# Retention scores with full-height matmuls: the queries' low parts kept per head beside rows of zeros

## The chip, the core and the metric

The kernel runs on one core of a Trainium2 chip. The metric is the device time of one execution in microseconds (us), as the median of several runs. The engines are named as the profile names them: PE is TensorE (matmuls), PEld its weight loads, DVE VectorE, ACT ScalarE, POOL GpSimd, SP the engine that issues the transfers.

## The reference

A model of three blocks over 512 tokens of width 1024: a layer of forgetting attention, a layer of retention, and a block of dilated attention, convolution and feed-forward. The change touches the retention alone, cut here to what matters (12 heads, keys and queries of 64, values of 128):

```python
qf = rotary(q.reshape(B, S, H, dk).astype(jnp.float32), pos)
kf = rotary(k.reshape(B, S, H, dk).astype(jnp.float32), pos) * (dk ** -0.5)
...
inner = jnp.einsum('bhnd,bhmd->bhnm', qc, kc) * d_inner[None]
o = jnp.einsum('bhnm,bhme->bhne', inner, vc)
```

The kernel computes the chunks' recurrence as one causal product over all 512 tokens: scores of every key block against the queries behind it, times a table of decays, then times the values.

## The kernel before

Every float32 product is made of float32r parts, a high part and a low part that holds the rest: hi by hi, hi by lo, lo by hi. The helper `mm3` writes these three matmuls (L213, L214, L215), and `add_nat` the same three in another layout (L422 to L424). Slots of 128 x 512 come from `arena_r` (50, float32r) and `arena_f` (23, float32), PSUM banks from a ring of eight; the slot that has been free longest is handed out first.

Jobs stand in a list, each with a tile of weights. Between two pieces of a job's foreground work (24 or 48 matmuls of a projection) the driver lets one or two steps of background chains run. A head of the retention is such a chain, `push_head`, with the steps `s1` (scores), `s2` (product with the values, by the helper `pv`), `s2b` (sums of squares, a small POOL power at L231, diagonal blocks at L251) and `s3` (the norm spread by two matmuls, L261 and L262, and the gate). A scheduler then orders the instructions of each engine.

A pair of heads shares one projected chunk. `store_rot` turns it by the rotary tables (ACT L1087, DVE L1088, POOL L1089, DVE L1090) and stores parts: of a key, for each head, the high part in the head's own 64 partitions with the low part in the other 64; of a query, for each head, the high part in both halves, and one slot for the low parts of both heads, each in its own 64 partitions. So the first matmul of a score block (L1127, 128 partitions) gives hi by hi and lo by hi at once, and the second (L1128) adds hi by lo over the head's 64 partitions alone. A group of scores is eight matmuls, four blocks of two: 512, 384, 256 and 256 columns. DVE multiplies each block with the decays (L1131, L1136), ACT makes its high part (L1132), POOL its low part (L1133), and `s2` reads them.

Of the kernel before, what the change touches and what calls it, by code (L numbers as in the profile page):

```python
# [11 lines left out]
F32 = mybir.dt.float32  # L12
# [28 lines left out]
class Slots:  # L41
    """Equal pieces of one on-chip buffer, handed out in program order, the longest free one first."""
# [26 lines left out]
class HL:  # L69
    """A float32 array held as the sum of two float32r arrays."""  # L70
# [10 lines left out]
class Job:  # L81
    """One weight tile: how to load it, how to cut its split, and the pieces of work that use it."""
# [6 lines left out]
class Chain:  # L89
    """Steps of background work, in order; one at most between two pieces of the foreground."""  # L90
# [10 lines left out]
def tile_kernel(ctx: ExitStack, tc: tile.TileContext, a: dict, out: bass.AP, stop_at=None):  # L101
    nc = tc.nc
# [21 lines left out]
    # ---------------------------------------------------------------- constants  # L124
# [53 lines left out]
    def vec_steps(r0, r1):  # L178
        """Rows r0 .. of the vectors, turned so that their elements lie on partitions, as steps."""
        n = r1 - r0  # L180
        d = {}

        def load():
            d["t"] = st = FS.get()
            r = 0
            while r < n:
                ap, i = vrows[r0 + r]
                m = 1
                while r + m < n and vrows[r0 + r + m] == (ap, i + m):
                    m += 1  # L190
                nc.sync.dma_start(st[r : r + m, 0:P], ap[i : i + m, :])
                r += m

        def turn():
            pt = PA.get()
            nc.tensor.transpose(pt[:, 0:n], d["t"][0:n, 0:P], ident[0:n, 0:n])
            nc.vector.tensor_copy(vec[:, r0:r1], pt[:, 0:n])
            pt.free()
            d["t"].free()

        return [load, turn]

    # ---------------------------------------------------------------- small helpers
# [4 lines left out]
    def mm3(ps, pairs, start=True, stop=True, check=True):  # L208
        """ps (+)= sum of w.T @ x, each float32 operand as hi + lo."""
# [7 lines left out]
    def stat_mm(ps4, src, first, last, blocks=range(4)):  # L217
        """ps4[t, i] += sum over partitions of src[:, 128 i + t]."""
# [14 lines left out]
    def bcast(ps, col4, n=4):  # L233
        """ps[:, t] = the value of token t, on every partition."""
        for i in range(n):
            nc.tensor.matmul(  # L236
                ps[:, i * P : (i + 1) * P],
                col4[:, i : i + 1].to_broadcast([P, P]),
                ident,
                start=True,  # L240
                stop=True,
            )

    def diag(col4):
        """Four diagonal blocks of the values of 512 tokens, split."""
# [13 lines left out]
    def bcast_r(ps, g):  # L259
        """ps[:, t] = the sum over the partitions of g[:, t], on every partition."""  # L260
# [4 lines left out]
    def norm_apply(xs, g0, rb, dst, cs=range(KC)):  # L265
        """dst[c] = split of xs[c] * g * rb."""
# [16 lines left out]
    # ---------------------------------------------------------------- the driver  # L283
# [22 lines left out]
    def pump():  # L306
        """Loads as far ahead as the buffers allow."""
# [8 lines left out]
    def cut(j):  # L316
        """The next piece of the split of j's weights into hi and lo."""
# [15 lines left out]
    def cut_ahead(i, n):  # L333
        """Up to n pieces of the split, of the tiles up to i + 2."""
# [47 lines left out]
    A = slice(None)  # L382
# [8 lines left out]
    def add_proj(w, c0, x, evacs, n=512):  # L391
        """Two 128-wide column chunks of x @ w, transposed; evacs[i](psum) stores chunk i."""
# [17 lines left out]
    def add_nat(w, c0, x, evac, nb=4, cut=None):  # L410
        """x @ w[:, c0:c0+256] in its natural layout; evac(b, psum) stores rows 256 b .. 256 b + 255."""
# [22 lines left out]
    def add_acc(w, r0, nr, ncols, xs, evac, cols=None):  # L434
        """Chunks of xs' rows r0.. of w: partial products of w's rows, transposed; evac(f, psum)."""
# [22 lines left out]
    # ---------------------------------------------------------------- attention pieces  # L458
    def softmax_T(blocks, dst):
        """Transposes of blocks: dst list of (psum column, source) per psum bank."""  # L460
# [4 lines left out]
    # ================================================================ phase: start  # L465
    G = {}

    def load_nat(src, nt, between=lambda: None):
        """[128 nt, 1024] in its natural layout: units [token block][column half]."""
# [8 lines left out]
    def nat_rstd(r, nt, act):  # L478
        """Root mean square of each row -> [128, 4] of 1 / rms."""
# [18 lines left out]
    def mem_steps(layer):  # L498
        """Split of mem * g, transposed, and 1 / rms of mem's rows, as steps."""
# [55 lines left out]
    def x_steps():  # L555
        """The residual and h, transposed, from x, as steps."""
# [41 lines left out]
    def sq_add(key, c, src, scale=1.0):  # L598
        """Sums of squares over the chunks."""
# [14 lines left out]
    def spread_to(key, col4):  # L614
        """Broadcast of [128, 4] to a unit."""
# [6 lines left out]
    def raw_split(c, g0):  # L622
        """Split of x * g, which still lacks 1 / rms."""
# [6 lines left out]
    def norm_steps(g0, key="sq", keep_rb=False):  # L630
        """New h from the residual x, whose squares are summed up, as steps."""
# [31 lines left out]
    # ================================================================ mem attention  # L663
# [45 lines left out]
    def store_q(key, first=None):  # L709
        """Split of a chunk; its first 128 tokens whole as well."""  # L710
# [98 lines left out]
    def add_out(layer, g, then=None):  # L809
        """Residual += o[4g .. 4g+3] @ w_out rows; then(f) follows each chunk."""  # L810
# [44 lines left out]
    # ================================================================ layer 0  # L855
    def add_fox():
# [3 lines left out]
        def ev_f(ps):  # L860
            """Cumulated log-sigmoid of the forget logits, times -sqrt(128), to DRAM."""
# [91 lines left out]
        def f_unit(h, l):  # L953
            """Rows 0 .. 31: products of hi and of x's lo; rows 32 .. 63: of the weights' lo, which lie beside hi."""
# [80 lines left out]
    def tr_causal(p, p33):  # L1035
        """p[i]: [128 queries of block i, keys 0 .. 128 (i + 1)], transposed and split.

        keys 0, queries 0:512; keys 1, queries 128:512; keys 2, queries 256:512, lo beside hi; p33: keys 3, whole."""
# [15 lines left out]
    def pv(v, odd, pt, p33):  # L1054
        """Output, transposed: sum over key blocks of v.T @ pt; the last block, 128 queries, as plain float32."""
# [13 lines left out]
    # ================================================================ layer 1  # L1069
    def add_ret():  # L1070
# [9 lines left out]
        def store_rot(key):  # L1080
            """Rotated pair of heads: a key's hi beside its lo, a query's hi twice; last the queries' lo."""

            def f(ps):
# [8 lines left out]
                n = 2 if key[0] == "k" else 3  # L1092
                G[key] = r = [RS.get() for _ in range(n)]
                for i in range(2):
                    own, other = HEADS[i], HEADS[1 - i]
                    nc.scalar.copy(r[i][own], t[own])
                    if n == 3:
                        nc.scalar.copy(r[i][other], t[own])
                    lo = r[i][other] if n == 2 else r[2][own]
# [7 lines left out]
        def push_head(h):  # L1107
# [5 lines left out]
            def s1():  # L1113
                q, k = G[("q", h // 2)], G[("k", h // 2)]
                rows = HEADS[h % 2]
                kh, qh, ql = k[h % 2], q[h % 2], q[2]
# [5 lines left out]
                for j in range(4):  # L1122
# [5 lines left out]
                    nc.tensor.matmul(ps[:, 0:n], kh[rows, sl], ql[rows, q0:512], start=False, stop=True)  # L1128
# [107 lines left out]
    # ================================================================ block 2  # L1236
# [10 lines left out]
    def bias_steps():  # L1247
        """Bias of every head by distance, masked distances at -1e30, reversed, times sqrt(128), to DRAM."""
# [41 lines left out]
    def mid_steps():  # L1290
        """h = rmsnorm(rmsnorm(x, final), mix_pre); then the inner norm, which is the residual, to DRAM."""
# [43 lines left out]
    def glu_evac(i, gate, val, c, raw):  # L1335
        """Gated value chunk c into a padded row; raw ones still lack h's 1 / rms."""
# [10 lines left out]
    def add_glu_raw():  # L1347
        """Chunks 0 and 1 of the gated value, from h without its 1 / rms."""
# [86 lines left out]
    def add_qk(g, j):  # L1435
        """Query and key chunk of head 4 g + j."""
# [33 lines left out]
    def by_residue(ap):  # L1470
        """Tokens 4 t + r of a row of 512 in the order of (r, t)."""
        return ap.rearrange("p (t r) -> p r t", r=4)

    def stats(j, g):
        """Row maxima (columns 0 .. 11) and sums (12 .. 23) of the three groups, for tokens in the order of group g."""
# [5 lines left out]
    def own_exp(g, j, p):  # L1481
        """Exponentials over the group's own maxima, and their sums."""
# [9 lines left out]
    def scores_dil(g, j):  # L1492
        """A dilated group attends within the tokens of equal residue by 4, in blocks of 128."""
# [41 lines left out]
    def push_softmax(j):  # L1535
        def swap():
            """Each order's maxima and sums to the other, by DRAM."""
# [12 lines left out]
        def coef(g):  # L1550
            """Columns 0 .. 11: exp(own maximum - joint maximum) over the joint sum."""
# [74 lines left out]
    def tr_band(p):  # L1626
        """p[0]: [128, keys 0]; p[i]: [128, keys i - 1, i].  Two split units of two key blocks each;
        key block j: queries 128 j .. 128 j + 255, the last one zeros and then queries 384:512."""
# [33 lines left out]
    def add_v2(g, jp):  # L1662
        """Values of two heads; those of a dilated group go through DRAM into the order of (residue, token)."""
# [24 lines left out]
    def conv_norm():  # L1688
        """LayerNorm over channels, silu and split of the convolution's output; pushed as background steps."""
# [53 lines left out]
    def add_block2():  # L1743
# [123 lines left out]
        def last(hf):  # L1867
            """Chunks 6 and 7 for 256 of the tokens."""
# [16 lines left out]
        def post(hf):  # L1885
            """The residual and its raw split, for 256 of the tokens."""
# [32 lines left out]
    # ================================================================ feed-forward  # L1919
    def add_ffn():  # L1920
# [38 lines left out]
        def add_up_raw():  # L1959
            """Chunks 0 to 3 of the gated unit, from h without its 1 / rms; the first four products side by side."""  # L1960
# [63 lines left out]
        def down(g, lo, n):  # L2024
            """y += f chunks lo .. lo + n - 1 times w_down's rows, in the natural layout."""
# [65 lines left out]
        def final(t, h, cs=A):  # L2091
            """Squares summed up, and the gain, for 128 tokens and half of the columns or less."""
# [18 lines left out]
        def final_out(t):  # L2111
            """out = x + rmsnorm(y) for 128 tokens."""
# [9 lines left out]
        def x_nat_steps():  # L2122
            """The residual in its natural layout."""
# [54 lines left out]
    # ================================================================ the program  # L2178
# [97 lines left out]
```

## Time and profile before

| | |
|---|---|
| median of 3 runs | 1933.24 us (1933.07 to 1943.24) |
| the profiled execution, first to last instruction | 1935.2 us |
| PE busy | 1880.0 us, 97% |
| DVE, ACT, POOL busy | 1133.0 us, 826.5 us, 361.5 us |
| instructions | 24633 |

The profile comes from one execution; its own time is the span of 1935.2 us, and no other time of it is given. Shares of busy time are means over stages with different limits, so the rows of the retention's own stretch matter more than the page's sums. Rows of matmuls overlap: how long one takes of PE's time is read from its start to the start of the next, not from its length.

### The profile page before, as it was taken

How to read it: one execution, taken by the hardware profiler on the slowest of the kernel's cores; microseconds unless marked ns; L12 is line 12 of the kernel's file. 1: busy time of each engine (PE TensorE's matmuls, PEld its weight loads, DVE VectorE, ACT ScalarE, POOL GpSimd, SP SyncE). 2: the span in 40 equal slices, each digit the busy share in tenths (PEclk: the TensorE clock that was granted, in tenths of full speed). 3: DMA queues.
4: the chain of work that ended last, by engine and by line, in shares of the span. 5: the costliest groups of instructions: out<-in, count | busy, mean ns of one | idle time of the engine just before them, and what ended most of it. 6: DMA issues, size and time to landing. Idle time of an engine off the chain costs nothing. (4 is left out here: it accounts for less than half of the span.)

```text
span 1935.2 us, 24633 instructions
## 1 busy us (share of the span) xinstructions
PE 1880.0 (97%) x9759; PEld 1594.7 (82%) x9759; DVE 1133.0 (59%) x1752; ACT 826.5 (43%) x1389; POOL 361.5 (19%) x348
## 2 busy tenths in 40 slices
PE   8999999999999999999999997999899999999998
PEld 7788888888888888888777986988788887888886
DVE  7644443443574564745469796868365387545555
ACT  6544343444445534445244333234353356433342
POOL 1110000111121223223351202020121232100101
PEclk9999999999999999999989998999999999999999
DMA  6341322223242222322223522353453222323221
GB/s 205 120 130 67 98 82 88 92 77 109 87 130 89 77 88 77 94 60 97 66 88 114 166 90 62 80 155 88 136 174 126 98 66 82 116 96 98 98 87 66
DMA packets 200373, 194.57 MB, mean 101 GB/s; under 512 B 22199, under 2 KB 171574, under 8 KB 200258
## 3 DMA queue, kind: packets, MB, share of 16 engines
q1 hardware_dynamic: 200258, 193.00, 32.0%
q8 instruction: 76, 1.25, 0.3%
q14 instruction: 39, 0.32, 0.1%
HBM read 182.40 MB, written 12.94 MB: 101 GB/s over the span
## 5 line engine op out<-in xcount | busy, mean ns | idle before, releaser
L213 PE MATMUL psum<-arena_r,ring_hl 128*128 128x512 f32 (+1 forms) x1936 | 750.1, 388 | 1.8 <-ACT arena_r L1904 1.3
L215 PE MATMUL psum<-arena_r,ring_hl 128*128 128x512 f32 (+1 forms) x1936 | 742.1, 384 | 5.1 <-DVE ring_hl L326 5.1
L214 PE MATMUL psum<-arena_r,ring_hl 128*128 128x512 f32 (+1 forms) x1936 | 742.5, 384 | 3.4 <-DVE arena_r L627 2.6
L326 DVE TENSOR_TENSOR ring_hl<-ring_w,ring_hl 128x1024 fp32r<-128x1024 f32 (+2 forms) x306 | 392.6, 1290 | 314.5 <-ACT ring_hl L324 303.6
L324 ACT CAST ring_hl<-ring_w 128x1024 fp32r<-128x1024 f32 (+2 forms) x307 | 316.1, 1037 | 504.3 <-PE psum L214 335.1
L215 PEld LDWEIGHTS psum<-arena_r,ring_hl 128*128 128x128 f32 x1936 | 367.1, 190 | 77.7 <-DVE ring_hl L326 6.3
L214 PEld LDWEIGHTS psum<-arena_r,ring_hl 128*128 128x128 f32 x1936 | 367.8, 190 | 73.7 <-DVE arena_r L627 3.3
L213 PEld LDWEIGHTS psum<-arena_r,ring_hl 128*128 128x128 f32 x1936 | 367.5, 190 | 73.1 <-issue 2.1
L422 PE MATMUL psum<-ring_hl,arena_r 128*128 128x256 f32 x640 | 183.3, 286 | 2.2 <-ACT ring_hl L324 2.2
L424 PE MATMUL psum<-ring_hl,arena_r 128*128 128x256 f32 x640 | 182.6, 285 | 0.3 <-DVE ring_hl L326 0.3
L423 PE MATMUL psum<-ring_hl,arena_r 128*128 128x256 f32 x640 | 182.5, 285 | 0.0
L1418 DVE SCALAR_TENSOR_TENSOR arena_f<-cpad,vec,arena_f 128x512 f32<-128x512 f32 x240 | 173.3, 751 | 1.7
L422 PEld LDWEIGHTS psum<-ring_hl,arena_r 128*128 128x128 f32 x640 | 124.2, 194 | 3.5 <-ACT ring_hl L324 2.6
L424 PEld LDWEIGHTS psum<-ring_hl,arena_r 128*128 128x128 f32 x640 | 124.1, 194 | 0.6 <-DVE ring_hl L326 0.6
L423 PEld LDWEIGHTS psum<-ring_hl,arena_r 128*128 128x128 f32 x640 | 124.1, 194 | 0.5
L206 DVE TENSOR_TENSOR arena_r<-psum,arena_r 128x512 fp32r<-128x512 f32 (+2 forms) x136 | 79.1, 605 | 71.3 <-ACT arena_r L205 71.1
L205 ACT CAST arena_r<-psum 128x512 fp32r<-128x512 f32 (+2 forms) x136 | 66.9, 526 | 85.0 <-PE psum L215 35.9
L205 ACT CAST arena_r<-arena_f 128x512 fp32r<-128x512 f32 (+1 forms) x78 | 46.2, 598 | 116.8 <-POOL arena_f L1950 67.3
L926 POOL TENSOR_SCALAR arena_f<-arena_f,small 128x512 f32<-128x512 f32 (+3 forms) x48 | 33.9, 726 | 307.9 <-DVE small L924 302.6
L206 DVE TENSOR_TENSOR arena_r<-arena_f,arena_r 128x512 fp32r<-128x512 f32 (+1 forms) x78 | 53.2, 688 | 59.8 <-ACT arena_r L205 59.1
L606 POOL TENSOR_TENSOR arena_f<-arena_f 128x512 f32<-128x512 f32 x40 | 63.6, 1602 | 109.1 <-ACT arena_f L601 106.8
L1950 POOL TENSOR_TENSOR arena_f<-arena_f 128x512 f32<-128x512 f32 x22 | 32.0, 1455 | 262.2 <-DVE arena_f L1926 252.2
(237 smaller groups left out, 2099.3 us busy)
## 6 DMA issues: line engine op xcount, KB each, us to landing
ring_w<-in_fox_w_in SPq DMA_DIRECT2D x28, 1024.0 KB
ring_w<-in_w_in SPq DMA_DIRECT2D x22, 1024.0 KB
ring_w<-in_w_up SPq DMA_DIRECT2D x22, 1024.0 KB
ring_w<-in_w_out SPq DMA_DIRECT2D x20, 1024.0 KB
ring_w<-in_ret_w_in SPq DMA_DIRECT2D x16, 1024.0 KB
ring_w<-in_w_in SPq DMA_DIRECT2D x24, 512.0 KB
ring_w<-in_w_down SPq DMA_DIRECT2D x10, 1024.0 KB
ring_w<-in_w_mem_kv SPq DMA_DIRECT2D x8, 1024.0 KB
```

The lines of the kernel that those rows point to most:

```text
L205: nc.scalar.copy(h, src)
L206: nc.vector.tensor_sub(l, src, h.bitcast(F32))
L213: nc.tensor.matmul(ps, wh, xh, start=start and k == 0, stop=False, **o)
L214: nc.tensor.matmul(ps, wh, xl, start=False, stop=False, **o)
L215: nc.tensor.matmul(ps, wl, xh, start=False, stop=stop and k == n - 1, **o)
L324: nc.scalar.copy(j.hv[sl], v[sl])
L326: (nc.gpsimd if j.done in j.spare else nc.vector).tensor_sub(lo, v[sl], j.hv[sl].bitcast(F32))
L422: nc.tensor.matmul(o, c.h[:, sl], h[:, k, :], start=k == 0, stop=False)
L423: nc.tensor.matmul(o, c.l[:, sl], h[:, k, :], start=False, stop=False)
L424: nc.tensor.matmul(o, c.h[:, sl], l[:, k, :], start=False, stop=k == n - 1)
L606: nc.gpsimd.tensor_add(acc, acc, t.ap)
L1418: nc.vector.scalar_tensor_tensor(t, src, wk, t, ALU.mult, ALU.add)
```

## The change

`store_rot` now takes four slots for a pair's queries instead of three: the low parts lie in a slot per head, in the head's own 64 partitions, and POOL writes zeros into the other 64 (L1099). The score step's second matmul then runs over all 128 partitions; the key's low part, which lies in the other half of its slot, meets the zeros and adds nothing. Nothing is computed that was not computed before. The number of matmuls and their columns stay.

```diff
-                n = 2 if key[0] == "k" else 3
+                n = 2 if key[0] == "k" else 4
                 G[key] = r = [RS.get() for _ in range(n)]
                 for i in range(2):
                     own, other = HEADS[i], HEADS[1 - i]
                     nc.scalar.copy(r[i][own], t[own])
-                    if n == 3:
+                    if n == 4:
                         nc.scalar.copy(r[i][other], t[own])
-                    lo = r[i][other] if n == 2 else r[2][own]
+                        nc.gpsimd.memset(r[2 + i][other].bitcast(F32), 0.0)
+                    lo = r[i][other] if n == 2 else r[2 + i][own]
                     nc.vector.tensor_sub(lo, t[own], r[i][own].bitcast(F32))
...
-                rows = HEADS[h % 2]
-                kh, qh, ql = k[h % 2], q[h % 2], q[2]
+                kh, qh, ql = k[h % 2], q[h % 2], q[2 + h % 2]
...
                     nc.tensor.matmul(ps[:, 0:n], kh[:, sl], qh[:, q0:512], start=True, stop=False)
-                    nc.tensor.matmul(ps[:, 0:n], kh[rows, sl], ql[rows, q0:512], start=False, stop=True)
+                    nc.tensor.matmul(ps[:, 0:n], kh[:, sl], ql[:, q0:512], start=False, stop=True)
```

The rest of the diff takes out comments. The numbers of lines stay but for L1100 to L1111, which move down by one: the low parts' subtraction is L1101 in the new kernel.

On PE nothing moves. This is the score group of the first head of the fourth pair with the matmul ahead of it and the one behind it, with the semaphores that each row waits for; these rows read the same in both programs (the height of a matmul is not printed).

```order
L215 MATMUL psum<-arena_r,ring_hl 128x512
L1127 MATMUL psum<-arena_r 128x512 [waits DVE_49]
L1128 MATMUL psum<-arena_r 128x512
L1127 MATMUL psum<-arena_r 128x384 [waits DVE_49]
L1128 MATMUL psum<-arena_r 128x384
L1127 MATMUL psum<-arena_r 128x256
L1128 MATMUL psum<-arena_r 128x256
L1127 MATMUL psum<-arena_r 128x256 [waits DVE_49]
L1128 MATMUL psum<-arena_r 128x256
L213 MATMUL psum<-arena_r,ring_hl 128x512 [waits Activation_49]
```

No row of PE waits for POOL because of the zeros: by the time a score group comes, PE has already waited for something that stands behind them on POOL.

On POOL the twelve zero fills are new. The first four stand ahead of the memory heads' normalising (L774), before the first pair's queries are turned (L1089); this is the difference there.

```order
 L326 TENSOR_TENSOR ring_hl<-ring_w,ring_hl 128x8x128
 L271 TENSOR_TENSOR arena_r<-arena_f,arena_r 128x512 x4
-L774 TENSOR_SCALAR arena_f<-arena_f,small 128x256 x12
+L1099 MEMSET arena_r 64x512 x2
+L774 TENSOR_SCALAR arena_f<-arena_f,small 128x256 x4
+L1099 MEMSET arena_r 64x512 x2
+L774 TENSOR_SCALAR arena_f<-arena_f,small 128x256 x8
 L1089 TENSOR_TENSOR arena_f<-arena_f 128x512 x2
```

They stand well ahead of the work that they belong to: two pairs' zeros are written before the first query is turned.

Further on in POOL's program, at the third and fourth pair, the old order of the low parts (L1133) and of the next turn (L1089) is this.

```order
L1133 TENSOR_TENSOR arena_r<-arena_f,arena_r 128x256
L1133 TENSOR_TENSOR arena_r<-arena_f,arena_r 128x512
L1133 TENSOR_TENSOR arena_r<-arena_f,arena_r 128x384
L1133 TENSOR_TENSOR arena_r<-arena_f,arena_r 128x256
L1089 TENSOR_TENSOR arena_f<-arena_f 128x512
L231 TENSOR_TENSOR small<-small,nhalf 128x4
L251 TENSOR_TENSOR arena_r<-ident,small 128x512 x2
L1089 TENSOR_TENSOR arena_f<-arena_f 128x512
```

And this is the new one at the same place.

```order
L1133 TENSOR_TENSOR arena_r<-arena_f,arena_r 128x256
L1133 TENSOR_TENSOR arena_r<-arena_f,arena_r 128x512
L1133 TENSOR_TENSOR arena_r<-arena_f,arena_r 128x384
L1133 TENSOR_TENSOR arena_r<-arena_f,arena_r 128x256
L1099 MEMSET arena_r 64x512 x2
L1089 TENSOR_TENSOR arena_f<-arena_f 128x512
L231 TENSOR_TENSOR small<-small,nhalf 128x4
L251 TENSOR_TENSOR arena_r<-ident,small 128x512 x2
L1089 TENSOR_TENSOR arena_f<-arena_f 128x512
```

Two zero fills now stand between a head's low parts and the next turn; they wait for PE to have read what their slots held before, last of all by an L262.

## Rows read from the trace of the kernel before

**Rows 1.** The page: the span, and the granted clock in 40 equal slices.

```profile
span 1935.2 us, 24633 instructions
PEclk9999999999999999999989998999999999999999
```

**Rows 2.** Busy time of PE, PEld, DVE, ACT, POOL in the retention; clock, DMA, GB/s.

```profile
630.00:960.00 330.00, 330.00 (x1701) 274.67 (x1699) 187.99 (x274) 150.54 (x237) 96.50 (x84) 0.98 0.26 82
```

**Rows 3.** Timeline of PE around one score group: start, us, engine, line, shapes.

```profile
652.09 0.48 PE L1127 MATMUL psum<-arena_r 128*128 128x512 f32 x1
652.50 0.49 PE L1128 MATMUL psum<-arena_r 64*128 64x512 f32 x1
652.92 0.44 PE L1127 MATMUL psum<-arena_r 128*128 128x384 f32 x1
653.29 0.44 PE L1128 MATMUL psum<-arena_r 64*128 64x384 f32 x1
653.66 0.38 PE L1127 MATMUL psum<-arena_r 128*128 128x256 f32 x1
653.98 0.38 PE L1128 MATMUL psum<-arena_r 64*128 64x256 f32 x1
...
654.91 0.50 PE L213 MATMUL psum<-arena_r,ring_hl 128*128 128x512 f32 x1
655.25 0.39 PE L214 MATMUL psum<-arena_r,ring_hl 128*128 128x512 f32 x1
...
655.94 0.39 PE L214 MATMUL psum<-arena_r,ring_hl 128*128 128x512 f32 x1
```

**Rows 4.** Timeline of PE in a head's product with the values, all 128 high.

```profile
662.54 0.33 PE L213 MATMUL psum<-arena_r 128*128 128x384 f32 x1
...
663.06 0.29 PE L213 MATMUL psum<-arena_r 128*128 128x256 f32 x1
...
663.43 0.38 PE L1064 MATMUL psum<-arena_f 128*128 128x128 f32 x2
```

**Rows 5.** Timeline of PEld: one weight load in the score group, one behind it.

```profile
652.50 0.18 PEld L1128 LDWEIGHTS psum<-arena_r 64*128 64x128 f32 x1 [0.24 <-issue]
...
655.25 0.19 PEld L215 LDWEIGHTS psum<-arena_r,ring_hl 128*128 128x128 f32 x1
```

**Rows 6.** PE busy in the ten stretches of score groups, with the clock: one and the sum.

```profile
719.95:727.03 7.08, 7.08 (x17) 0.73 0.41 140
...
sum 34.84, PE 34.84; mean PE 3.48
```

**Rows 7.** PE busy and granted clock where it fell in the retention.

```profile
723.00:730.20 7.20, 7.20 (x16) 0.53 0.19 57
839.00:843.00 4.00, 4.00 (x11) 0.57 0.27 66
927.90:931.60 3.70, 3.70 (x10) 0.54 0.00 0
```

**Rows 8.** Timelines of DVE, POOL and PE behind the scores of the ninth head.

```profile
913.85 1.48 DVE L1131 TENSOR_TENSOR arena_f<-psum,arena_f 128x512 f32<-128x512 f32 x3
...
915.26 2.96 POOL L1133 TENSOR_TENSOR arena_r<-arena_f,arena_r 128x512 fp32r<-128x512 f32 x3 [5.77 <-ACT arena_r L1132]
...
918.28 0.39 PE L214 MATMUL psum<-arena_r 128*128 128x256 f32 x1
```

**Rows 9.** POOL's groups by line: the fill with the most elements per partition.

```profile
L879 POOL MEMSET arena_f<- 12x512 f32 x1 | 0.5, 517 | 13.6 <-PE psum L196 13.6
```

**Rows 10.** Timelines of PE, POOL and DVE from an L262 to the fourth pair's scores.

```profile
743.32 0.39 PE L262 MATMUL psum<-arena_r,ones_r 128*128 128x512 f32 x1
...
746.62 1.30 POOL L1089 TENSOR_TENSOR arena_f<-arena_f 128x512 f32<-128x512 f32 x1 [18.42 <-ACT arena_f L1087]
...
756.84 1.40 DVE L1100 TENSOR_TENSOR arena_r<-arena_f,arena_r 64x512 fp32r<-64x512 f32 x2
...
766.90 0.39 PE L1127 MATMUL psum<-arena_r 128*128 128x512 f32 x1
```

## The prediction

> **What bounds the kernel now.** I read the page first: the profiled execution spans 1935.2 us, 2.0 us above the median of the runs (1933.24), so I work out a difference in the trace and take it off the median [rows 1]. Then the busy times of the stretch in which the retention's heads run, from 630 to 960 us: PE is busy for 330.00 of 330.00 us, DVE for 188, ACT for 151, POOL for 97 [rows 2]. PE waits for nobody there, so a microsecond that it needs less is a microsecond off the time, unless some other engine then lets it wait.
>
> Next, PE's timeline through one score group. The reader is to look at starts, not lengths. Its first pair of 512 columns starts at 652.09 and 652.50, the next matmul at 652.92: 0.41 and 0.42 us apart. The 384 columns follow at 0.37, the 256 columns at 0.32 [rows 3]. Foreground matmuls of 512 columns behind it go at 655.25 to 655.94 in three steps, 0.23 us each [rows 3]. In the product with the values, all of it 128 high, three matmuls of 384 columns take 0.52 us, 0.173 each, and three of 256 take 0.37, 0.123 each [rows 4]. So each of the eight score matmuls costs some 0.19 us more than its columns do elsewhere.
>
> The weight loads say what that is. In the foreground the load for L215 starts at 655.25, together with the matmul before it. In the score group the load of L1128 starts at 652.50, when its own matmul starts, and PEld stood idle for 0.24 us before it [rows 3, 5]. A load takes 0.18 to 0.19 us [rows 5], and 0.23 + 0.19 = 0.42, 0.173 + 0.19 = 0.36, 0.123 + 0.19 = 0.31 are the starts seen. What I conclude: where a matmul of 64 rows and one of 128 alternate, the next weights aren't loaded under the running matmul. The price falls on both kinds, and on the first foreground matmul behind the group: 654.91 to 655.25 is 0.34, 0.11 above 0.23 [rows 3].
>
> Last, the clock. In the retention it fell to 0.5 (1.2 GHz) three times. By the windows' means, 7.20 x (1 - 0.53) x 2 = 6.8 us, then 3.4 and 3.4 us ran at half speed [rows 7]. Each began inside or at the end of a score group or a double one.
>
> **The change part by part.**
>
> *The groups.* At full height a group should stream at the foreground's pace: 2 x 0.23 + 2 x 0.173 + 4 x 0.123 = 1.30 us. Twelve take 15.6 us. Today the ten stretches (two hold two heads' groups) sum to 34.84 us [rows 6]. Gain 19.2 us. Their ten exits give 10 x 0.11 = 1.1 us.
>
> Bounds of this term: nothing if weights stay exposed for another reason, 20.3 us if all goes. I take the whole: L1127 and L1128 read the same kind of slots, with as many columns, as the matmuls of rows 4, and nothing but the height differs.
>
> *The clock.* Of the 13.6 us at half speed, 7.08 x (1 - 0.73) x 2 = 3.8 lie inside the double group at 719.95, whose excess is in the term above [rows 6, 7]. The other 9.7 us hold foreground work at half speed, half of which is lost: 4.9 us. Bounds: nothing, if the falls stay, or 4.9 us. What PE did before each fall was a score group; packed into 1.30 us, two in a row 2.6 us, it looks like foreground. I take the 4.9.
>
> *A gain that is lost again.* Behind the ninth head's scores DVE takes up the products with the decays only at 913.85, being busy with the next pair's turn; POOL's low parts then end at 915.26 + 2.96 = 918.22, and PE's L214, which reads the last, starts at 918.28 [rows 8]. PE arrives exactly with POOL now. It would arrive 1.5 us earlier and wait, because DVE's queue there isn't started by this group. Loss: one group's gain, 2.8 (34.84 / 12 is 2.90, less the slow one's share) - 1.3 = 1.5 us.
>
> *The zero fills.* Twelve on POOL, 64 x 512. The nearest row is a fill of 12 x 512 at 517 ns [rows 9]; a far upper bound is POOL's product of 128 x 512 at 1.30 us [rows 10]. I take 0.52 us, since 512 elements per partition are the same: 6.2 us in all, within POOL's 330 - 97 = 233 idle us [rows 2]. The tightest place is the fourth pair, where two fills wait for an L262 that ends at 743.71 and POOL is next needed at 746.62 for L1089: 2.9 us for 1.04 [rows 10]. At 1.30 us each they'd still fit. If they didn't, L1089, L1090 and the subtraction behind them, which ends at 758.24, would be late, and the scores that read it start only at 766.90 [rows 10]. So: nothing. Behind the fills on POOL stand L774, L1133 and L1089 alone; no transfer is issued from there. SP's order is unchanged, and the fourth slot per pair only shifts which slot comes next. PE's rows have no new wait.
>
> *DVE and ACT* do the same instructions on the same shapes.
>
> *Sum:* 19.2 + 1.1 + 4.9 - 1.5 = 23.7 us; 1933.2 - 23.7 = **1909.5 us**, 1.2% less.
>
> **A rule against it.** What rows 5 show is a load that runs under a full-height matmul when the next is full-height too. The Trainium skill's "TensorE: Matmul & The Clock Gate", section "The mechanism" (row and column tiling), says otherwise: a weight load overlaps a matmul in flight only when the row groups differ. By that rule the eight full-height matmuls, all on the same rows, would each show its load and nothing would be won, about 1933 us. The trace disagrees with it here: 0.23 us per foreground matmul of 512 columns leaves no room for an exposed load of 0.19.
>
> **The rivals.**
>
> *The falls of the clock stay.* For it: at 927.9 the group came behind work of other kinds, and it may be that which let the clock fall. Against: all three falls lie at groups [rows 6, 7]. Time: 1909.5 + 4.9 = 1914.4 us.
>
> *Other engines become the bound in the double groups.* DVE needs 1.48 us for three products [rows 8] and a fourth beside them, more than PE's 1.30. With two heads in a row all eight PSUM banks are filled in 2.6 us, and what comes next waits for DVE. The four heads' gain of 4 x 1.5 = 6 us would go: 1915.5 us. Against: the next piece needs one bank, and the first product frees one early.
>
> *Loads stay exposed.* Should the cause be not the height but what the two lines share, their slots or two loads of the same weights, nothing comes: 1933 us. Against: L213 and L214 also load the same weights twice, at 0.23 us.
>
> *Slower: the fills hold up POOL.* Each pair's two fills would have to take 2.9 us plus the 766.90 - 758.24 = 8.7 us of slack, 11.6 us together, before PE waits at all; from 15.6 us a pair (7.8 each) on, six pairs eat the 23.7 us. At 8.5 us each: 1909.5 + 6 x 5.4 = 1942 us. The row says 0.52 [rows 9], so only a behaviour that no row shows would do it.
>
> **How the numbers follow.** As forecast 0.60; the clock's falls stay 0.17; waits on DVE 0.13; no gain 0.06; slower 0.04. The forecast's own range reaches down by the ninth head's 1.5 and by some 5 us, the size of this term of the clock, because the falls later in the span (slices 21 and 25 [rows 1]) may come or go as the stream moves: 1903. Upwards it takes in both rivals that still gain, with a little of each together: 1918. A measurement of this kernel tells about 0.5%, 9.7 us, from no change. Faster by more than that: 0.60 + 0.17 + 0.13 = 0.90, and 0.01 of a partly exposed load, 0.91; the same 0.06; slower 0.03.
>
> **What would show it right or wrong.** Right: in the new timeline of PE the starts of a score group lie 0.23, 0.17 and 0.12 us apart and the foreground behind it goes on at 0.23; the ten stretches sum to about 16 us; the clock stays near 1.00 from 630 to 940; the fills' rows read about 0.5 us; PE shows a wait of about 1.5 us for POOL's L1133 at the ninth head. Wrong: starts still 0.4 and 0.3 apart with all rows 128 high, waits of PE on DVE's L1131 behind a double group, half-speed stretches elsewhere that eat the gain, or fills of several us ahead of L1089.

## The result

The changed kernel takes 1917.6 us (median of 4 runs, 1914.26 to 1920.95) against 1933.15 for the kernel before (4 runs, 1933.02 to 1943.24). The two medians lie 15.6 us apart, 0.8%; the ratio on record is 0.9899, 95% interval 0.9876 to 0.9923, and is not the quotient of the two medians. In a longer comparison it was 1916.65 (4 runs, 1913.48 to 1917.41) against 1938.61 (23 runs, 1932.54 to 1949.30), ratio 0.9879 (0.9852 to 0.9906), or 22.0 us less. The kernel before differs from run to run by up to 0.9%, the changed one by up to 0.4%, and the median of a few runs of the kernel before is known to about 5 us.

So it is faster, by 1.0 to 1.2% by the recorded ratios. The forecast of 1909.5 was 8.1 us too low; the range's upper end, 1918, just holds the result.

**The profile after.** The page's span and clock, to set beside [rows 1]:

```profile
span 1912.5 us, 24641 instructions
...
PE 1855.5 (97%) x9759; PEld 1587.8 (83%) x9759; DVE 1134.0 (59%) x1752; ACT 825.5 (43%) x1389; POOL 368.2 (19%) x360
...
PEclk9999999999999999999999998999999999999999
```

The span is 22.7 us shorter. PE's busy time is 24.5 us less, with the same number of matmuls; DVE and ACT stand still, and POOL has 12 instructions and 6.7 us more.

PE's timeline in the first score group, as in [rows 3] (start, us, engine, line, shapes):

```profile
653.05 0.48 PE L1127 MATMUL psum<-arena_r 128*128 128x512 f32 x1
653.37 0.40 PE L1128 MATMUL psum<-arena_r 128*128 128x512 f32 x1
653.60 0.34 PE L1127 MATMUL psum<-arena_r 128*128 128x384 f32 x1
653.78 0.34 PE L1128 MATMUL psum<-arena_r 128*128 128x384 f32 x1
653.95 0.28 PE L1127 MATMUL psum<-arena_r 128*128 128x256 f32 x1
654.07 0.28 PE L1128 MATMUL psum<-arena_r 128*128 128x256 f32 x1
...
654.43 0.40 PE L213 MATMUL psum<-arena_r,ring_hl 128*128 128x512 f32 x1
654.67 0.40 PE L214 MATMUL psum<-arena_r,ring_hl 128*128 128x512 f32 x1
```

The starts are 0.23, 0.18, 0.17 and 0.12 us apart where they were 0.42 to 0.31. The first step, 0.32, is 0.09 longer than the rest: ahead of it stand transposes of 128 columns (L782), and not another product. The exit, from 654.43 to 654.67, is 0.24 where it was 0.34.

The weight loads of the same group, as in [rows 5]:

```profile
653.14 0.19 PEld L1128 LDWEIGHTS psum<-arena_r 128*128 128x128 f32 x1
653.37 0.19 PEld L1127 LDWEIGHTS psum<-arena_r 128*128 128x128 f32 x1
```

The load for the L1128 that starts at 653.37 starts at 653.14, under the L1127 ahead of it. Before, it began when its own matmul did.

Windows of PE busy and clock: the whole retention, as in [rows 2], and the ten score stretches, as in [rows 6].

```profile
630.00:960.00 330.00, 328.15 (x1801) 1.00 0.27 85
```

```profile
717.77:720.35 2.58, 2.58 (x18) 1.00 1.02 349
...
sum 15.77, PE 15.77; mean PE 1.58
```

The ten stretches take 15.8 us instead of 34.8. The double group that took 7.08 us at a clock of 0.73 takes 2.58 at 1.00, and the clock is 1.00 all through the retention in this execution (before 0.98, with three falls [rows 7]). PE is no longer busy the whole time: 1.85 us of 330 are idle. The list of PE's waits from 640 to 960 us names nearly all of it (engine, line, who was waited for, us in total, times, longest):

```profile
PE psum L214 <- POOL arena_r L1133: 1.8, 2, 0.9
```

It is the place of [rows 8], whose head the prediction numbered the ninth: it is the eighth of the ten stretches, two of which are double, so the head is the tenth (h = 9). PE, DVE and POOL there:

```profile
897.65 0.50 PE L213 MATMUL psum<-arena_r 128*128 128x512 f32 x1
899.00 0.50 PE L214 MATMUL psum<-arena_r 128*128 128x512 f32 x1 [0.85 <-POOL arena_r L1133]
...
901.64 0.38 PE L214 MATMUL psum<-arena_r 128*128 128x256 f32 x1 [0.93 <-POOL arena_r L1133]
...
902.12 0.48 PE L213 MATMUL psum<-arena_r,ring_hl 128*128 128x512 f32 x1
```

```profile
896.26 1.48 DVE L1131 TENSOR_TENSOR arena_f<-psum,arena_f 128x512 f32<-128x512 f32 x3
...
897.67 3.92 POOL L1133 TENSOR_TENSOR arena_r<-arena_f,arena_r 128x512 fp32r<-128x512 f32 x3 [5.77 <-ACT arena_r L1132]
```

In the kernel before, the product's first matmul and the first foreground matmul behind it are these:

```profile
916.66 0.40 PE L213 MATMUL psum<-arena_r 128*128 128x512 f32 x1
...
918.77 0.48 PE L213 MATMUL psum<-arena_r,ring_hl 128*128 128x512 f32 x1
```

DVE still takes up the products late, 5.8 us behind the start of the score group in both kernels. PE comes to the product with the values 1.4 us sooner behind that start than before (897.65 - 890.47 = 7.2 us against 916.66 - 908.09 = 8.6) and waits for the low parts twice. From the product to the foreground are 902.12 - 897.65 = 4.47 us, before 918.77 - 916.66 = 2.11, so 2.4 us are lost here.

The three subtractions also took longer, 3.92 us against 2.96 [rows 8]. The trace puts that on the third alone, of 256 columns: 1.71 us against 0.74, while the first two took 1.27 and 1.02 against 1.29 and 1.02. DVE was at a piece of the weights' split (L326) when the third one began, at 899.88; before, that piece began with the third one (917.49). First the changed kernel, then the kernel before:

```profile
899.29 1.71 DVE L326 TENSOR_TENSOR ring_hl<-ring_w,ring_hl 128x1024 fp32r<-128x1024 f32 x1 [1.36 <-ACT ring_hl L324]
```

```profile
917.51 1.80 DVE L326 TENSOR_TENSOR ring_hl<-ring_w,ring_hl 128x1024 fp32r<-128x1024 f32 x1 [1.98 <-ACT ring_hl L324]
```

Of the changed kernel's twelve third subtractions seven took 0.74 us; the three that took 1.7 us all began while an L326 was running, the two that took 1.2 while an L1101 was. That they go together is seen; no run tests that the one slows the other.

### The profile page after: what moved, and what is told of

It is laid out like the page before. It is cut to its first block, busy times and chain, and to the rows that moved or that the text cites. A ratio compares the mean times of both kernels' runs of the same rounds, so it can differ in the third digit from the quotient of the medians.

```text
span 1912.5 us, 24641 instructions
## 1 busy us (share of the span) xinstructions
PE 1855.5 (97%) x9759; PEld 1587.8 (83%) x9759; DVE 1134.0 (59%) x1752; ACT 825.5 (43%) x1389; POOL 368.2 (19%) x360
## 5 line engine op out<-in xcount | busy, mean ns | idle before, releaser
L326 DVE TENSOR_TENSOR ring_hl<-ring_w,ring_hl 128x1024 fp32r<-128x1024 f32 (+2 forms) x306 | 394.6, 1296 | 303.0 <-ACT ring_hl L324 297.8
```

Of the source, the lines that this page charges most:

```text
L326: (nc.gpsimd if j.done in j.spare else nc.vector).tensor_sub(lo, v[sl], j.hv[sl].bitcast(F32))
```

## The experiments

**The spread between runs.** First, both kernels unchanged, with many runs.

> The kernel before once more, unchanged. Theory (the clock's falls differ from one execution to the next, and the profiled execution had more of them than the median): its times spread by a few us with the mean granted clock, each 0.001 of clock being worth about 1.9 us, and the falls in its trace within the retention may number fewer than three, or lie elsewhere. Rival (the falls are fixed, always three there): the trace shows the three falls of 723, 839 and 928 us again, and the times differ by under 1 us.

> The changed kernel once more. Theory: twelve score groups sum to 15.8 us again, no fall of the clock starts in them, and the times spread from 1914 to 1921 us as the mean clock spreads from 0.990 to 0.984, by falls outside the retention. Rival (the slower executions have the retention's falls back): falls between 630 and 940 us in the trace of a slower execution.

The kernel before: 1939.79 us (12 runs, 1933.21 to 1945.38), a ratio of 1.0004 (0.9987 to 1.0022) to the 23 other runs of the same kernel. Its profiled execution spans 1942.0 us, 6.8 more than the first one. Windows at the three falls of [rows 7], which come here 4.5 us later:

```profile
727.00:735.00 8.00, 8.00 (x18) 0.57 0.24 75
843.00:848.00 5.00, 5.00 (x15) 0.66 0.29 68
932.00:937.00 5.00, 5.00 (x15) 0.66 0.00 2
```

Worked out as in the prediction, that is 8 x (1 - 0.57) x 2 = 6.9, 3.4 and 3.4 us at half speed: the same three falls of the same sizes at the same groups. The span's extra time isn't from them. It goes with the clock in the rest of the span: the mean clock is 0.982 against 0.985, and 0.003 of 1942 us is 5.8 of the 6.8 us (an estimate). Over the 23 runs it's alike, from 1932.54 us at 0.987 to 1949.30 at 0.979. So the theory is right on the spread and the rival on the three falls.

The changed kernel again has ten stretches of 15.8 us, but in this execution the clock fell once in the retention, right behind the tenth head's waits. It was the fastest of its four (1913.48 us), so the rival, falls in the slower ones, isn't borne out by it:

```profile
901.00:905.00 4.00, 3.76 (x12) 0.57 0.32 96
```

**What in the height costs.** The kernel before, with a group's four full-height matmuls first and then its four of 64 rows: as many of each, but two changes of height, one in the group and one behind it, in place of eight.

```diff
-                    nc.tensor.matmul(ps[:, 0:n], kh[:, sl], qh[:, q0:512], start=True, stop=False)
-                    nc.tensor.matmul(ps[:, 0:n], kh[rows, sl], ql[rows, q0:512], start=False, stop=True)
+                banks = [PA.get() for _ in range(4)]
+                for low in range(2):
+                    for j in range(4):
+                        if low:
+                            nc.tensor.matmul(ps[:, 0 : 512 - q0], kh[rows, sl], ql[rows, q0:512], start=False, stop=True)
+                        else:
+                            nc.tensor.matmul(ps[:, 0 : 512 - q0], kh[:, sl], qh[:, q0:512], start=True, stop=False)
```

> The kernel before, with 64-row matmuls as they were, but the four full-height matmuls of a group first and then its four 64-row ones: two changes of height in a group and its exit, instead of eight. Theory (each change of height costs one weight load that nothing covers, 0.19 us): a group takes 1.30 + 0.19 = about 1.5 us and its exit 0.1 more than usual, so the ten stretches sum to about 18 us; few or no falls of the clock; 12 to 18 us less than before. Rival 1 (a 64-row matmul costs more by itself, wherever it stands): the group stays at about 2.7 us and the time is that of before. Rival 2 (the drain is longer than a load): a group of 1.7 us or more.

1920.42 us (4 runs, 1919.24 to 1922.05), ratio 0.9898 (0.9874 to 0.9922). PE's timeline of the second group (L1131 is the full-height matmul there, L1129 the one of 64 rows, four in a row each), the weight loads at the two changes of height, and the sum of the ten stretches:

```profile
668.64 0.80 PE L1131 MATMUL psum<-arena_r 128*128 128x512 f32 x4
669.38 0.91 PE L1129 MATMUL psum<-arena_r 64*128 64x512 f32 x4
670.21 0.49 PE L213 MATMUL psum<-arena_r,ring_hl 128*128 128x512 f32 x1
670.55 0.39 PE L214 MATMUL psum<-arena_r,ring_hl 128*128 128x512 f32 x1
```

```profile
669.37 0.70 PEld L1129 LDWEIGHTS psum<-arena_r 64*128 64x128 f32 x4
670.21 0.19 PEld L213 LDWEIGHTS psum<-arena_r,ring_hl 128*128 128x128 f32 x1
```

```profile
sum 19.33, PE 19.33; mean PE 1.93
```

At full pace four blocks need 0.23 + 0.17 + 0.12 + 0.12 = 0.64 us. The four of 128 rows take 0.74, the four of 64 rows 0.83, and the exit 0.34 instead of 0.23. So a change of height costs about 0.20 us: 0.09 on the last matmul ahead of it and 0.11 on the first behind it. At each change the load starts only with its own matmul (669.37 and 669.38, 670.21 and 670.21). The four loads of L1129 are over after 0.70 us, at 670.07, while their matmuls hold PE until 670.21: behind the first they run under the matmuls. So 64-row matmuls one behind the other run as fast as full ones: the 0.83 less both parts of the price is 0.63. That fits the old group too: with a change at every matmul each pays both parts, some 0.19 to 0.20. The rival that a matmul of 64 rows is dear in itself falls. The other one, that two loads of the same weights in a row matter, isn't tested here, as no two such loads stand in a row any more; it falls with the changed kernel, which still has them and runs at full pace. The group, 1.57 us, and the sum came out somewhat above the 1.5 and 18 expected.

The Trainium skill's "TensorEngine Tiling (Array Packing)", section "Key Properties", says that a change of the tiling mode drains TensorE; it gives no price. These rows agree that the change costs time, and the price is the 0.20 us; whether the array is emptied in it they don't tell.

**The storage alone.** The changed kernel's four slots and its zeros, with the second matmul still over the head's 64 rows, so that the zeros are written and never read. Against the kernel before:

```diff
-                n = 2 if key[0] == "k" else 3
+                n = 2 if key[0] == "k" else 4
...
+                        nc.gpsimd.memset(r[2 + i][other].bitcast(F32), 0.0)
+                    lo = r[i][other] if n == 2 else r[2 + i][own]
...
                     nc.tensor.matmul(ps[:, 0:n], kh[rows, sl], ql[rows, q0:512], start=False, stop=True)
```

> One part of the change alone: four slots for a pair's queries and the zero fills, but the second matmul still over the head's 64 rows, so that the zeros are written and never read. Theory (the height is the whole gain, the storage costs nothing): the ten stretches sum to 33 to 35 us again with starts 0.42, 0.37 and 0.31 us apart, the clock falls at the score groups again, and the time is that of the kernel before, 1933 to 1945 us. Rival (part of the gain comes from the slots in another order): 1925 us or less.

1938.05 us (12 runs, 1932.65 to 1945.81), ratio 1.0006 (0.9989 to 1.0023). The last two of its stretches, and the sum:

```profile
930.65:933.98 3.33, 3.33 (x10) 0.80 0.08 26
950.69:953.72 3.03, 3.03 (x11) 0.91 0.00 0
sum 34.76, PE 34.76; mean PE 3.48
```

The slow groups are back, and so are falls of the clock at them. The whole gain hangs on the height; the slots and zeros alone neither win nor lose more than the ratio's interval, 0.2% or some 4 us.

**The price of the zeros.** The changed kernel, each fill written twice.

```diff
                         nc.gpsimd.memset(r[2 + i][other].bitcast(F32), 0.0)
+                        nc.gpsimd.memset(r[2 + i][other].bitcast(F32), 0.0)
```

> The changed kernel with every zero fill written twice, 24 instead of 12. Theory (the fills lie in idle time of POOL and cost nothing): POOL is busy 6.3 us more, the groups still sum to 15.8 us, the time is that of the changed kernel, 1913 to 1921 us. Rival (the fills already hold up POOL where the next turn waits for it): up to 6 us more, with PE waiting for something that stands behind a fill.

1917.72 us (4 runs, 1915.42 to 1920.17), ratio 0.9889 (0.9863 to 0.9914): no different from the changed kernel. POOL's groups of fills (busy, mean ns | idle before):

```profile
L1099 POOL MEMSET arena_r<- 64x512 f32 x12 | 6.3, 521 | 27.1 <-PE psum L214 15.6 <-PE psum L261 8.6 <-PE psum L215 2.3
L1100 POOL MEMSET arena_r<- 64x512 f32 x12 | 6.2, 520 | 0.7
```

A fill takes 0.52 us, POOL idles 27 us for PE ahead of them, and doubling them leaves the ten stretches at 15.8 us and PE's waits at 1.8 us in all. They are hidden.

**The clock with the alternating groups kept.** The kernel before, with each odd head's chain begun one place later, so that no two heads' groups stand together.

```diff
-            return [s1, s2, s2b] + [nop] * early + [s3]
+            return [nop] * (h % 2) + [s1, s2, s2b] + [nop] * early + [s3]
```

> The kernel before, with 64-row matmuls in the old order, but the odd heads' chains start one step later, so that no two score groups stand back to back. Theory (the long stretch of drained matmuls lets the clock fall, the double groups above all): the sum of the groups stays at 12 x 2.73 = 33 us, the falls at the two double groups go, and the time is 3 to 6 us under before. Rival (the falls come from elsewhere, or single groups make them as well): as many falls in the retention as before and a time within 2 us of before.

1942.51 us (11 runs, 1941.39 to 1946.16), ratio 1.0014 (0.9999 to 1.0028). Windows, and the waits of PE from 600 to 1075 us that grew most:

```profile
560.00:600.00 40.00, 37.35 (x183) 0.91 0.41 127
600.00:960.00 360.00, 358.23 (x1864) 1.00 0.27 84
960.00:1075.00 115.00, 106.56 (x514) 0.96 0.30 88
```

```profile
PE psum L214 <- DVE arena_r L627: 4.2, 2, 2.5
...
PE psum L262 <- POOL arena_r L251: 1.6, 2, 1.4
PE psum L261 <- POOL arena_r L251: 1.5, 1, 1.5
```

Both expectations missed. The three falls are gone with all the groups still of mixed heights, at single groups too; so the alternation isn't enough to bring a fall. The time didn't follow. The later chains let PE idle for 1.8 + 8.4 = 10.2 us from 600 to 1075 us, 5.3 before (475 less the 469.67 busy): 4.9 us of new waits. And a fall stands at 560 to 600 us (0.91) where the clock was 1.00; the kernel with the storage alone has one there too (0.91), so it need not come from this edit. This run shows that the falls can be avoided with the heights still alternating; what that is worth it doesn't show.

**The gain that is lost again.** Four kernels, two of them at the wrong head for the slip in numbering named above. The first two delay `s2` by one place, or move the low parts from POOL to DVE, for h = 8.

```diff
+            return [s1] + [nop] * (h == 8) + [s2, s2b] + [nop] * early + [s3]
```

```diff
+                        (nc.vector if h == 8 else nc.gpsimd).tensor_sub(outs[j][1], t[:, 0:n], outs[j][0].bitcast(F32))
```

> The changed kernel with one empty step between the ninth head's scores and its product with the values, so that PE comes to POOL's low parts a piece of foreground work later. Theory (PE's three waits there cost 2.2 us against the kernel before, and nothing else is late): the waits of PE for POOL's L1133 go and 2 us are won, unless the later chain makes PE wait at the retention's end. Rival (DVE's backlog there moves along): the wait stays at about 3 us.

> The changed kernel with the ninth head's three low parts taken by DVE, at 0.4 to 0.7 us each, instead of POOL, which took 3.9 us for them. The order of PE and ACT stays. Theory (PE waits there for POOL's pace behind DVE's late products): the low parts end some 2 us earlier, PE's waits shrink from 3 to about 1 us, and the time is 2 us less, 1912 to 1918 us. Rival (the wait is ACT's or DVE's own lateness): PE still waits about 3 us, now for DVE.

`ninth_later`: 1916.65 us (5 runs, 1914.02 to 1920.45), ratio 0.9887 (0.9861 to 0.9913). The waits for L1133 went all the same, but PE waits 0.7 and 0.3 us for POOL's L251 ahead of L261 and L262. `ninth_on_dve`: 1918.62 us (4 runs, 1916.02 to 1920.94), ratio 0.9893 (0.9868 to 0.9918); the 1.8 us of waits stay, as the wrong head was moved, and the clock falls behind them:

```profile
897.20:903.20 6.00, 4.80 (x16) 0.72 0.09 31
```

Neither tests the place that was meant. The same two edits for h = 9 do:

> The changed kernel with three low parts on DVE instead of POOL once more, now for the head behind whose scores PE really waits: the stretch at 890 us is the eighth of ten, but two stretches hold two heads, so that it is the tenth head's; the two runs named after the ninth moved the head before it. Theory: DVE takes 0.4 to 0.7 us for a low part where POOL took 0.9 to 1.7, PE's waits there shrink from 3 to about 1 us, the fall of the clock behind them goes, and the time is 2 to 4 us less, 1911 to 1917 us. Rival (ACT's high parts or DVE's own backlog are late): PE waits as long as before, now for DVE.

> The changed kernel with one empty step between the tenth head's scores and its product with the values. Theory: PE meets POOL's low parts a piece of foreground work later and doesn't wait there, but everything behind it in the last heads comes a step later, so that what is won, about 2 to 3 us, is partly given back by waits for POOL's L251 at the end of the retention. Rival (no cost at the end): 2 to 4 us less.

`tenth_on_dve`: 1914.34 us (4 runs, 1914.05 to 1920.04), ratio 0.9890 (0.9873 to 0.9907). The rows of PE and DVE that answer to those of the changed kernel:

```profile
895.77 0.49 PE L213 MATMUL psum<-arena_r 128*128 128x512 f32 x1
896.51 0.50 PE L214 MATMUL psum<-arena_r 128*128 128x512 f32 x1 [0.24 <-DVE arena_r L1133]
...
898.10 0.47 PE L213 MATMUL psum<-arena_r,ring_hl 128*128 128x512 f32 x1
```

```profile
895.77 1.49 DVE L1133 TENSOR_TENSOR arena_r<-arena_f,arena_r 128x512 fp32r<-128x512 f32 x3
```

From the product's first matmul to the foreground behind it are 2.33 us; in the changed kernel 902.12 - 897.65 = 4.47. So 2.1 of the 2.4 us lost at this place come back, and POOL's low parts are the cause. The median is 2.3 us under the changed kernel's second one, the lowest of all that were run, but its four runs overlap with those, and its profiled span, 1912.5, is that of the changed kernel's first profile. A gain over the changed kernel isn't shown.

`tenth_later`: 1917.94 us (4 runs, 1917.65 to 1918.04), ratio 0.9901 (0.9887 to 0.9915). The wait for L1133 went and another came, no gain:

```profile
PE psum L261 <- POOL arena_r L251: 0.7, 1, 0.7
PE psum L262 <- POOL arena_r L251: 0.3, 1, 0.3
```

## Why the prediction was right, and where it was off

**The groups (19.2 us): right.** 34.84 - 15.77 = 19.07. The starts are the 0.23, 0.17 and 0.12 foretold. The cause, the change of height, is shown in both directions: by the storage alone, which keeps the height and gains nothing, and by the regrouping, which gets back 34.8 - 19.3 = 15.5 us with the 64-row matmuls kept. The conclusion from the loads, that the next weights aren't loaded under the running matmul where heights alternate, holds at both changes of the regrouped kernel; its price is 0.20 us per change, about one load (0.19).

**The exits (1.1 us): right**, 0.34 to 0.24.

**The clock (4.9 us): right in the retention** of the first profile, where it is 1.00. In the second profile of the changed kernel 3.4 us at half speed stand there, 1.7 us of the 4.9 lost again. The rival that the falls stay, at the groups, did not happen. Why they came is less clear than the prediction had it: it laid them to the groups' shape, and the kernel with odd heads put off kept the shape and lost the falls.

**The gain lost again (1.5 us): right in place and mechanism, mis-sized.** It is 2.4 us (4.47 - 2.11): the 1.4 us that PE came earlier, and 1.0 because POOL's three subtractions took 3.92 us and not the 2.96 that the prediction left as they were.

**The fills (nothing) and the rivals.** 0.52 us each, and doubled they change nothing. DVE doesn't hold PE up behind a double group: no such wait is in PE's list. Loads don't stay exposed. The Trainium skill's "TensorE: Matmul & The Clock Gate", section "The mechanism", has a sentence that lets a load overlap a matmul in flight only when the row groups differ. The rows of the changed group contradict it: all are on the same rows, and the loads run under the matmuls. The same section also names loads into a background weight buffer as pulled ahead, which the prediction left out and these rows don't contradict.

**The sum.** From the first score matmul to the end of the last group, before and after:

```profile
946.51 0.50 PE L213 MATMUL psum<-arena_r,ring_hl 128*128 128x512 f32 x1
```

```profile
925.28 0.40 PE L213 MATMUL psum<-arena_r,ring_hl 128*128 128x512 f32 x1
```

946.51 - 652.09 [rows 3] = 294.4 us, and 925.28 - 653.05 = 272.2: 22.2 us less. The terms as found give 19.1 + 1.0 + 4.9 - 2.4 = 22.6 (the 4.9 as worked out in the prediction); 0.4 us is unassigned. The rest of the span adds 0.5, together the 22.7 us between the two profiles, against 23.7 forecast.

**The step that failed is the subtraction at the end**, "I work out a difference in the trace and take it off the median". The difference held; the median of three runs didn't stand for the kernel. The prediction read the span of 1935.2 as 2.0 us above it. But an execution lasts 1.8 us longer than its span (1914.26 to 1912.5 for the changed kernel, 1943.81 to 1942.0 for the kernel before), so the profiled one took about 1937.0, 3.8 us more than the median. And 23 runs put the median at 1938.61, another 17 at 1936.48, 9 at 1940.87. Of the 8.1 us of error 5.4 are the base (1938.6 - 1933.2; 3.2 and 7.6 by the medians of 17 and 9 runs), 1.7 the difference (23.7 - 22.0), and 0.9 lies between the two medians of the changed kernel. That the range still holds 1917.6, by 0.4 us, is luck: its upper end was set for rivals that did not happen, not for a base that was too low.

## What to carry to other kernels

Look at the heights in a row of matmuls, not at their columns alone: if short and full ones alternate, either fill the short ones up with zeros (here 12 fills of 0.52 us in POOL's idle time bought 19 us on TensorE) or put the like ones together, which gets most of it. When the bound engine gets faster, look for the places where it arrived just in time before; there it now waits. And a difference from one profile is taken off that execution's own time, with what lies around its span (1937.0 - 23.7 = 1913.3 here; the changed kernel's profiled run took 1914.26), or off a median of many runs, not of three.

## What the runs showed of the hardware

A change of matmul height costs 0.09 us ahead of it and 0.11 behind; this is seen in the regrouped kernel, and eight of them make up the old group's price.

In the retention of the kernels that are faster than before, the clock fell only where PE had waited twice for the tenth head's low parts. Such waits (1.6 to 1.8 us in all) stand in five of the profiles, and a stretch at half speed lies behind them in four: the changed kernel's second profile and `ninth_on_dve` above, and these windows of the doubled fills and of the regrouped kernel.

```profile
903.00:908.00 5.00, 4.16 (x14) 0.66 0.34 109
```

```profile
904.00:909.00 5.00, 4.48 (x15) 0.66 0.43 137
```

It does not lie there in the changed kernel's first profile, nor in any of the three kernels that took the waits away. So such waits go with a loss of 1.7 us more, half of a stretch of 3.4, in four of five profiles; that they let the clock fall is argued from this, not shown. What decides it is open, as is why the falls of the kernel before came at its groups and not in the kernel with odd heads put off. Open too is whether a DVE L326 in progress is what makes POOL's subtraction of 256 columns take 1.7 us instead of 0.74, as the rows above suggest.
